# Mixers of a two-block network: the input is normalised once ahead of the projections, the matrix-memory mixer divides no more, and three products move to GpSimd

## The chip, the cores and the metric

The kernel runs on one core of one Trainium2 chip. A core has five engines, which the profile calls PE (TensorE; its weight loads are listed apart as PEld), DVE (VectorE), ACT (ScalarE), POOL (GpSimd) and SP (SyncE, which here issues the DMAs). Each engine works through its own instructions strictly in the order in which they were written, and waits on semaphores for the others. The metric is the device time of one execution in microseconds (us).

## What is computed

Two blocks of two layers each work on 256 tokens of width 1024, in float32. The change touches the mixers of the first block, which stand between two feed-forward layers in each of its two layers:

```python
u = rms_norm(x, mix_norm[l]) @ w_in[l]          # x * rsqrt(mean(x*x) + EPS) * g
u_ssd, u_ml, u_rw = jnp.split(u, ...)
y_ssd = ssd_mixer(u_ssd, ...)      # silu(conv(xbc)); y_diag = einsum(cb * decay_ls, x_dt); y * silu(z)
y_ml  = mlstm_mixer(u_ml, ...)     # h = num / max(|den|, exp(-m_t)); group_rms_norm(h * o, norm_g, H)
y_rw  = rwkv7_mixer(u_rw, ...)     # us = uf + (u_prev - uf) * shift_mu; decays, a = sigmoid(...), k, kk
x = x + jnp.concatenate([y_ssd, y_ml, y_rw], axis=-1) @ w_out[l]
```

The norm has no mean to subtract, so its factor for one token, `rsqrt(mean(x*x) + EPS)`, may be applied to x before the product with `w_in` or to each column of the product after it. Likewise the head's own norm in the mLSTM makes a factor per token on `h` cancel, but for EPS.

## The kernel before

Everything is laid out with features on the 128 partitions and the 256 tokens along them. A product with float32 accuracy is three products of rounded halves (`mm3`): each operand is split into a high and a low part (`wh`, `wl` of a weight tile, `xh`, `xl` of x), and `wh*xh + wh*xl + wl*xh` is summed in PSUM, so one output tile of 128 features by 256 tokens takes 24 matmuls (8 slices of the width, 3 each). A weight tile `wr` comes by DMA; ACT rounds it to `wh` (line 145, CAST), DVE subtracts it to `wl` (line 146). Three tiles `wh`, `wl` may stand ready.

`win` runs through the columns of `w_in` tile by tile. `prod` multiplies one tile into an accumulator; there are three accumulators `acc` in PSUM (`K.n_acc, K.n_m, K.n_pn = 3, 5, 0`), used in turn, so the fourth tile can begin when the first one's accumulator has been read. What reads it is code of the mixer concerned:

- 14 tiles for the RWKV mixer go through `shift`: DVE multiplies the product by `rb` (the norm's factor per token, broadcast to all partitions; tile `cvy`), ACT scales a copy by one token's shift (`pad`), DVE combines them (`cvt`, `kr` or `v`). The first two tiles are `wlal` and `sg`, then come k, r, v of four groups of heads;
- 10 tiles for the SSD and 4 for the mLSTM go through `conv` (`rb` into `pad` or `xm`, four taps, silu as `(tanh + 1) * y` with tanh in `cvt` and y in `cvy`);
- one narrow tile goes to `rows`, 8 tiles to `sz` (silu of z) and 4 to `o` (tanh).

x in `xh`, `xl` carries the gain but not `rb`: `rb` is known only when the norm's sums over all of x are, so the first product starts without it.

Beside `win`, in steps that are taken between its tiles, run the generators `rwkv` (`rwkv_prep`: decays, keys and the products `bk`, with `kf` on POOL; then the inverse in `rwkv_main`, with score matrices `A4`), then `ssd` and `mlstm`. In `ssd`, for each of eight pairs of heads f, `mask(f)` makes the decay scores (`rw,sel` and `negr,identr` on PE, four exponentials `sd<-m,na` of 128x128 on ACT, and the product with `cbT`, `sd<-sd,cbT` of 128x512), and `out(f)` the result (`sd,xdt` and `ec,st` on PE, `sy` on DVE, the gate `sz<-sy,sz` on POOL, its square `sq` on ACT, the sum `sacc` on POOL). Two tiles `sd` exist. In `mlstm`, the denominator is summed by a matmul with a matrix of ones, so that it stands on all 128 partitions, and is then made the divisor by max, reciprocal and product.

No scheduler moves instructions: the order on every engine is the order in which the generators are advanced. The two mixer stages lie at about 204 to 489 us (layer 0) and 864 to 1152 us (layer 1).

Of the kernel before, what the change touches and what calls it, by code (L numbers as in the profile page):

```python
# [10 lines left out]
F32R = mybir.dt.float32r  # L11
# [5 lines left out]
T = 256  # L17
# [3 lines left out]
EPS = 1e-6  # L21
# [182 lines left out]
class Kernel:  # L204
# [220 lines left out]

    def rows(self, l, ps, rb, S):

        with self.tc.tile_pool(name=f"rows{l}", bufs=1, reuse_waits="tile") as P:
            yield from self.rows_(l, ps, rb, S, P)
        S["rows"] = True  # L430

    def rows_(self, l, ps, rb, S, P):
        nc, PA = self.nc, self.p_ph
# [4 lines left out]
        n, h16, h4 = slice(0, 68), slice(0, 16), slice(0, 4)  # L438
        self.tt(x[n], ps[n], rb[n], ALU.mult)
        self.act(li[h4], x[32:36], AF.Identity, bias=self.col(f"bias{l}")[32:36])  # L440
        self.ts(x[n], x[n], self.col(f"bias{l}")[n], self.col("sgn")[n], ALU.add, ALU.mult)
        yield from wait(3)
# [65 lines left out]
        nc.vector.tensor_tensor_scan(mx[h4, 128:256], g[h4, 128:256], g[h4, 128:256], mp[h4], op0=ALU.max, op1=ALU.max)  # L508
        R4 = self.sb(P, [128, 640], "r4")
        self.ts(R4[h4, 0:256], mx[h4], -1.0, None, ALU.mult)  # L510
        self.tt(bc[h4], bc[h4], mx[h4], ALU.add)
        self.act(R4[h4, 256:512], bc[h4], AF.Exp, scale=-1.0)
        self.act(R4[h4, 512:640], mx[h4, 128:256], AF.Exp, scale=-1.0, bias=mp[h4])
        Rs = self.sb(self.p_ph, [128, 640], "r4s", 1, F32R)
        nc.gpsimd.memset(Rs.bitcast(F32), 0.0)
# [4 lines left out]
    def win(self, l, xh, xl, rb, S):  # L520
# [49 lines left out]
        rows = self.rows(l, S["ps"], rb, S)  # L570
        next(rows)
# [6 lines left out]
        for i in range(8):  # L578
            yield from prod()
            ps = S["ps"]  # L580
            th = self.sb(P, [128, T], "cvt", 2)
            u = self.sb(P, [128, T], "cvy", 2)
            self.tt(u, ps, rb, ALU.mult)
            self.act(th, u, AF.Tanh, scale=0.5)
            self.stt(S["sz"][:, i, :], th, 1.0, u, ALU.add, ALU.mult)
            yield
# [7 lines left out]
        for i in range(4):  # L594
            yield from prod()
            self.conv(l, 10 + i, S["ps"], rb, S["xm"][:, i, :], S["xc"][:, i, :])
            yield
        for i in range(4):
            yield from prod()
            u = self.sb(P, [128, T], "cvy", 2)  # L600
            self.tt(u, S["ps"], rb, ALU.mult)
            self.act(S["o"][:, i, :], u, AF.Tanh, scale=0.5)
            yield


    def ssd(self, l, S):
# [6 lines left out]
        with self.tc.tile_pool(name=f"ssd{l}", bufs=1, reuse_waits="tile") as P:  # L613
# [51 lines left out]
            def mask(f):  # L665
# [69 lines left out]
    def mlstm(self, l, S):  # L735
# [6 lines left out]
        with self.tc.tile_pool(name=f"ml{l}", bufs=1, side="right", reuse_waits="tile") as P:  # L742
# [4 lines left out]
            def s1(h):  # L747
                ps = self.misc()
                sel = self.sel[:, h:h + 1].to_broadcast([128, 128])
                self.mm(ps, sel, R4[:, 0:512], True, False)  # L750
                self.mm(ps[:, 0:256], self.identr, self.negr, False, True)
                wT = self.sb(P, [128, 2, 128], "wT")
                for c in range(2):
                    self.act(wT[:, c, :], ps[:, 128 * c:128 * c + 128], AF.Exp, bias=gc[:, c, h:h + 1])
                eb = self.sb(P, [128, T], "eb", 2)
                nc.scalar.copy(out=eb, in_=ps[:, 256:512])
                ps = self.misc()
# [119 lines left out]
    def rwkv_prep(self, l, S, PA, P):  # L877
# [12 lines left out]
        def prep(i):  # L890
# [58 lines left out]
    def rwkv_main(self, l, S, PA, P):  # L949
# [198 lines left out]
    def mixers(self, l, xh, xl, rb, feed):  # L1148
# [12 lines left out]
        with ExitStack() as es:  # L1161
# [869 lines left out]
```

## Time and profile before

| | before |
|---|---|
| median of 3 runs | 3082.5 us (3082.49 to 3082.59) |
| the profiled execution | 3082.42 us, of which the trace's span is 3080.7 us |
| PE busy | 3023.4 us, 98% of the span |
| DVE / ACT / POOL busy | 2173.9 us (71%) / 1255.4 us (41%) / 119.0 us (4%) |
| granted clock of TensorE, mean | 0.992 of full speed |

The 1.7 us between the profiled time and the span lie before the first and behind the last instruction of the trace. Busy times are sums of what the engines did; whether time is lost is told by PE's waits, since PE is busy nearly all the time.

### The profile page before, as it was taken

What the parts mean: (1) busy time and instruction counts of PE and PEld (TensorE: products, weight loads), DVE (VectorE), ACT (ScalarE), POOL (GpSimd) and SP (SyncE); (2) the same over time, 40 slices, a digit from 0 to 9 for tenths busy, and PEclk for the clock granted to TensorE, in tenths of its full rate; (3) what the DMA queues carried; (4) which work ended last, traced back from release to release, by engine and by line L of the source; (5) the groups of instructions that cost most, each with busy time, mean ns of one, the idle gap of its engine ahead of it and who ended that gap; (6) DMA issues with size and microseconds to landing.
All of it is one profiled execution on the core that took longest, in us unless ns stands there. A gap on an engine that the chain in (4) does not pass through costs nothing.

```text
span 3080.7 us, 53271 instructions
## 1 busy us (share of the span) xinstructions
PE 3023.4 (98%) x21561; PEld 2738.5 (89%) x21561; DVE 2173.9 (71%) x3726; ACT 1255.4 (41%) x2096; POOL 119.0 (4%) x192
## 2 busy tenths in 40 slices
PE   8999999999999999999999999999999999999998
PEld 8998989999998999988888888888888887899898
DVE  8989777767678778758988657886533336566665
ACT  5453455444453555532222442222322224444443
POOL 0000120000010210000000000000000001100000
PEclk9999999999999999999999999999999999999999
DMA  8773335565542335545755224664223223333455
GB/s 289 245 245 100 101 111 175 175 195 185 175 157 64 117 124 185 186 140 172 230 192 184 77 83 161 212 203 143 95 88 104 91 84 131 103 122 105 145 182 147
DMA packets 138487, 463.69 MB, mean 151 GB/s; under 512 B 15360, under 2 KB 15616, under 8 KB 137984
## 3 DMA queue, kind: packets, MB, share of 16 engines
q1 hardware_dynamic: 138240, 460.29, 46.4%
q8 instruction: 169, 2.77, 0.4%
q14 instruction: 78, 0.64, 0.1%
HBM read 459.18 MB, written 1.05 MB: 149 GB/s over the span
## 4 chain that ended last, share of the span: by engine, by line
PE 86%; issue 7%; DVE 3%; ACT 2%; POOL 1%; DMA 0%; POOLq 0%; SPq 0%; DVEq 0%; ACTq 0%
PE acc L214 80%; PE m L214 5%; ACT wh L145 1%; DVE wl L146 1%; PE pn L214 0%; POOL nr L228 0%; POOL rr L228 0%; DVE bk L225 0%; DVE sm L904 0%; POOL kf L228 0%; POOL sz L228 0%; DVE xl L225 0%; DVE sd L228 0%; DVE bk L228 0%; DMA wr<-gu 0%
## 5 line engine op out<-in xcount | busy, mean ns | idle before, releaser
L145 ACT CAST wh<-wr 128x1024 fp32r<-128x1024 f32 (+2 forms) x794 | 762.0, 961 | 1436.7 <-issue 710.4
L214 PE MATMUL acc<-xh,wh 128*128 128x256 f32 (+2 forms) x3776 | 1192.0, 318 | 13.6 <-ACT wh L145 10.0
L146 DVE TENSOR_TENSOR wl<-wr,wh 128x1024 fp32r<-128x1024 f32 (+2 forms) x794 | 885.2, 1115 | 441.6 <-ACT wh L145 440.1
L214 PE MATMUL acc<-xh,wl 128*128 128x256 f32 (+2 forms) x3776 | 1188.8, 316 | 3.6 <-DVE wl L146 3.6
L214 PE MATMUL acc<-xl,wh 128*128 128x256 f32 (+2 forms) x3776 | 1188.5, 315 | 0.6 <-DVE xl L225 0.6
L214 PEld LDWEIGHTS acc<-xh,wh 128*128 128x128 f32 (+1 forms) x3776 | 712.1, 190 | 70.2 <-ACT wh L145 10.8
L214 PEld LDWEIGHTS acc<-xh,wl 128*128 128x128 f32 (+1 forms) x3776 | 714.8, 189 | 56.8 <-DVE wl L146 5.0
L214 PEld LDWEIGHTS acc<-xl,wh 128*128 128x128 f32 (+1 forms) x3776 | 715.6, 190 | 52.0 <-DVE xl L225 1.1
L214 PE MATMUL acc<-hh,wh 128*128 128x256 f32 (+1 forms) x1537 | 491.7, 320 | 0.0
L214 PE MATMUL acc<-hh,wl 128*128 128x256 f32 (+1 forms) x1537 | 491.6, 320 | 0.0
L214 PE MATMUL acc<-hl,wh 128*128 128x256 f32 (+1 forms) x1537 | 491.6, 320 | 0.0
L389 DVE CUSTOM_DVE_ANT_0 adaj<-adaw,silur,cols 128x1024 bf16<-128x1024 f32 x288 | 368.5, 1279 | 10.9 <-DMA adaw<-ada 8.7
L214 PEld LDWEIGHTS acc<-hl,wh 128*128 128x128 f32 x1537 | 289.2, 188 | 24.1
L214 PEld LDWEIGHTS acc<-hh,wh 128*128 128x128 f32 x1537 | 289.2, 188 | 24.1
L214 PEld LDWEIGHTS acc<-hh,wl 128*128 128x128 f32 x1537 | 289.2, 188 | 23.9
L228 DVE TENSOR_TENSOR fh<-fh,acc 128x512 f32<-128x512 f32 (+1 forms) x88 | 54.6, 620 | 153.0 <-PE acc L214 152.0
L235 ACT CAST hh<-fh 128x256 fp32r<-128x256 f32 (+1 forms) x176 | 84.9, 482 | 22.4 <-DVE fh L228 21.3
L228 DVE TENSOR_TENSOR hl<-fh,hh 128x256 fp32r<-128x256 f32 (+1 forms) x176 | 91.2, 518 | 3.1 <-ACT hh L235 3.1
L228 POOL TENSOR_TENSOR nr<-nv,mhalf 128x2 f32<-128x2 f32 x18 | 16.7, 926 | 1873.6 <-DVE nv L232 616.1
L228 DVE TENSOR_TENSOR fgu<-acc,rb 128x256 f32<-128x256 f32 x176 | 66.4, 418 | 25.4 <-PE acc L214 25.4
L225 DVE SCALAR_TENSOR_TENSOR x<-acc,gg,x 128x256 f32<-128x256 f32 x56 | 27.0, 482 | 52.7 <-PE acc L214 52.7
L222 ACT ACTIVATE xh<-nf,m 128x256 fp32r<-128x256 f32 x88 | 41.6, 504 | 48.8 <-DVE nf L225 48.8
(417 smaller groups left out, 2980.7 us busy)
## 6 DMA issues: line engine op xcount, KB each, us to landing
wr<-gu SPq DMA_DIRECT2D x352, 512.0 KB, 3.5
adaw<-ada SPq DMA_DIRECT2D x144, 512.0 KB, 4.3
wr<-dn SPq DMA_DIRECT2D x128, 384.0 KB, 3.1
wr<-dn SPq DMA_DIRECT2D x128, 320.0 KB, 3.0
wr<-win SPq DMA_DIRECT2D x80, 512.0 KB, 3.5
wr<-rin SPq DMA_DIRECT2D x48, 512.0 KB, 3.5
wr<-wout SPq DMA_DIRECT2D x32, 512.0 KB, 3.5
wr<-rout SPq DMA_DIRECT2D x16, 512.0 KB, 3.5
```

The lines of the kernel that those rows point to most:

```text
L145: self.nc.scalar.copy(out=hi[:, 0:n], in_=t[:, 0:n])
L146: self.nc.vector.tensor_sub(out=lo[:, 0:n], in0=t[:, 0:n], in1=hi[:, 0:n].bitcast(F32))
L214: self.nc.tensor.matmul(out=out, lhsT=lhsT, rhs=rhs, start=start, stop=stop)
L222: self.nc.scalar.activation(out=out, in_=in_, func=func, **k)
L225: return self.nc.vector.scalar_tensor_tensor(out, in0, scalar, in1, op0=op0, op1=op1)
L228: return (eng or self.nc.vector).tensor_tensor(out, in0, in1, op=op)
L235: self.nc.scalar.copy(out=hi, in_=full)
L389: self.nc.vector.tensor_tensor_reduce(out=junk, in0=w, in1=self.silur[:, s, :], scale=0.5, scalar=b, op0=ALU.mult, op1=ALU.add, accum_out= ...
```

## The change

1. `normalise`, called behind the first product of `win`, writes normalised x, split into `xnh`, `xnl`: for each of the 8 slices one DVE product (x times gain times `rb`, tile `cvy`), one ACT rounding and one DVE subtraction. From the fifth tile on (the first v tile) the products read `xnh`, `xnl`, and the product with `rb` behind them is left out; where ACT or DVE read `cvy` before, they read the accumulator. In `conv` an ACT copy puts the product into `pad`.
2. In `conv`, silu's last product is an ACT pass (tanh + 1) and a POOL product in place of one DVE instruction.
3. The product `sd<-sd,cbT` and the two `bk<-kf,sm` go from DVE to POOL.
4. In the mLSTM the sum of the denominator is a matmul with one column of ones (tokens on partitions), `r4s` is 384 wide in place of 640, `exp(-m_t)` is transposed once for all heads (`ebc`), and `den` goes into the EPS of the head's norm, scaled, in place of dividing.
5. `A4` takes the places of `xh`, `xl`.

```diff
-    def conv(self, l, i, ps, rb, pad, dst):
+    def conv(self, l, i, ps, pad, dst):
...
-        self.tt(pad[:, 3:259], ps, rb, ALU.mult)
-        ps = pad[:, 3:259]
+        nc.scalar.copy(out=pad[:, 3:259], in_=ps)
...
-        self.stt(dst, th, 1.0, y, ALU.add, ALU.mult)
+        self.act(th, th, AF.Identity, bias=1.0)
+        self.tt(dst, th, y, ALU.mult, eng=nc.gpsimd)
...
     def shift(self, l, i, ps, rb, dst):
...
-        us = self.sb(self.p_ph, [128, T], "cvy", 2)
-        self.tt(us, ps, rb, ALU.mult)
+        us = ps
+        if rb is not None:
+            us = self.sb(self.p_ph, [128, T], "cvy", 2)
+            self.tt(us, ps, rb, ALU.mult)
...
+        xn = [self.sb(self.p_xn, [128, 8, T], t, 1, F32R) for t in ("xnh", "xnl")]
+        def normalise():
+
+            for k in range(8):
+                f = self.sb(P, [128, T], "cvy", 2)
+                self.stt(f, self.x[:, k, 0:T], self.col(f"mix_norm{l}", k), rb, ALU.mult, ALU.mult)
+                self.split(f, xn[0][:, k, :], xn[1][:, k, :])
+
...
+        x_ = xh, xl
         yield from prod()
+        normalise()
         us = self.sb(P, [128, T], "cvt", 2)
         self.shift(l, 12, S["ps"], rb, us)
...
             for dst, j in ((S["kr"][:, i, :, 0, :], 4 + i), (S["kr"][:, i, :, 1, :], i), (S["v"][:, i, :], 8 + i)):
+                if (i, j) == (0, 8):
+                    x_, rb = [[t[:, k, :] for k in range(8)] for t in xn], None
                 yield from prod()
...
-                self.tt(d, d, cbT[:, :, f // 4, :].unsqueeze(1).to_broadcast([128, 2, 2, 128]), ALU.mult)
+                self.tt(d, d, cbT[:, :, f // 4, :].unsqueeze(1).to_broadcast([128, 2, 2, 128]), ALU.mult, eng=nc.gpsimd)
...
-                self.mm(ps, sel, R4[:, 0:512], True, False)
+                self.mm(ps[:, 0:256], sel, R4[:, 0:256], True, False)
...
-                    o = slice(256 + 128 * c, 384 + 128 * c)
-                    self.mm(ps[:, o], self.cst("ones"), s["p"][:, c, :], True, c == 0)
+                    o = slice(256 + c, 257 + c)
+                    self.mm(ps[:, o], s["p"][:, c, :], self.cst("ones")[:, 0:1], True, c == 0)
...
-                nc.vector.reciprocal(den, den)
-                self.tt(den, den, ps[:, 0:256], ALU.mult)
-                self.stt(hs[:, h, :], S["o"][:, h, :], 1.0, den, ALU.add, ALU.mult)
+                self.stt(vs[:, 2 * h:2 * h + 2], den, 4 * EPS, den, ALU.mult, ALU.mult)
+                self.stt(hs[:, h, :], S["o"][:, h, :], 1.0, ps[:, 0:256], ALU.add, ALU.mult)
...
-                self.tt(bk[half[e], i, :, 1 - e, :], r4(kf)[half[e]], r4(em)[half[e]], ALU.mult)
+                self.tt(bk[half[e], i, :, 1 - e, :], r4(kf)[half[e]], r4(em)[half[e]], ALU.mult, eng=nc.gpsimd)
...
-        A4 = [self.sb(P, [128, 2, 2, 4, 128], t) for t in ("A0", "A1")]
+        A4 = [self.sb(self.p_x, [128, 2, 2, 4, 128], t) for t in ("xh", "xl")]
```

Where the instructions stand now. On DVE, at the start of the mixers of layer 0, where `nv` is the norm's variance and the next line the first weight tile behind it, before:

```order
L232 TENSOR_SCALAR nv<-m 128x2
L146 TENSOR_TENSOR wl<-wr,wh 128x1024
L228 TENSOR_TENSOR cvy<-acc,rb 128x256
L225 SCALAR_TENSOR_TENSOR cvt<-cvy,omm_120,pad 128x256
L228 TENSOR_TENSOR cvy<-acc,rb 128x256
```

and of the change, from the same `wl`:

```order
L146 TENSOR_TENSOR wl<-wr,wh 128x1024
L225 SCALAR_TENSOR_TENSOR cvy<-x,cols,rb 128x256 x2
L228 TENSOR_TENSOR xnl<-cvy,xnh 128x256 x2
L225 SCALAR_TENSOR_TENSOR cvy<-x,cols,rb 128x256 x2
L146 TENSOR_TENSOR wl<-wr,wh 128x1024
L228 TENSOR_TENSOR xnl<-cvy,xnh 128x256 x2
L225 SCALAR_TENSOR_TENSOR cvy<-x,cols,rb 128x256 x2
L146 TENSOR_TENSOR wl<-wr,wh 128x1024
L228 TENSOR_TENSOR xnl<-cvy,xnh 128x256 x2
L225 SCALAR_TENSOR_TENSOR cvy<-x,cols,rb 128x256 x2
L228 TENSOR_TENSOR xnl<-cvy,xnh 128x256 x2
L228 TENSOR_TENSOR cvy<-acc,rb 128x256 x2
```

All of `normalise` stands ahead of the first `cvy<-acc,rb`, which reads the accumulator of the first tile. On POOL, in the SSD of layer 0, before:

```order
L228 TENSOR_TENSOR xde<-xdt,de 128x512 x2
L228 TENSOR_TENSOR sz<-sy,sz 128x256 x2
L228 TENSOR_TENSOR sacc<-sacc,sq 128x256
L228 TENSOR_TENSOR sz<-sy,sz 128x256
L228 TENSOR_TENSOR sacc<-sacc,sq 128x256
```

and of the change, to the sixth head pair's product:

```order
L228 TENSOR_TENSOR sd<-sd,cbT 128x512 x2
L228 TENSOR_TENSOR sz<-sy,sz 128x256
L228 TENSOR_TENSOR sd<-sd,cbT 128x512
L228 TENSOR_TENSOR sz<-sy,sz 128x256
L228 TENSOR_TENSOR sacc<-sacc,sq 128x256
L228 TENSOR_TENSOR sz<-sy,sz 128x256
L228 TENSOR_TENSOR sd<-sd,cbT 128x512
L228 TENSOR_TENSOR sacc<-sacc,sq 128x256
L228 TENSOR_TENSOR sd<-sd,cbT 128x512
L228 TENSOR_TENSOR sz<-sy,sz 128x256
L228 TENSOR_TENSOR sacc<-sacc,sq 128x256
L228 TENSOR_TENSOR sd<-sd,cbT 128x512
```

The products `sd` stand between the gates `sz` and sums `sacc` of earlier pairs. On ACT the exponentials for the sixth pair (the second row of four) stand behind the square of the fourth pair's gate:

```order
L222 ACTIVATE sd<-m,na 128x128 x4
L222 ACTIVATE sq<-sz 128x256
L222 ACTIVATE sd<-m,na 128x128 x4
L222 ACTIVATE sacc<-sz 128x256
L222 ACTIVATE o<-acc 128x256
L145 CAST wh<-wr 128x1024
L222 ACTIVATE sd<-m,na 128x128 x4
```

ACT keeps this order of squares and exponentials from before; what is new is that POOL's gates and sums and the products `sd` are one queue.

## Rows read from the trace of the kernel before

**Rows 1.** The page: busy times by engine, and the granted clock in 40 slices.

```profile
PE 3023.4 (98%) x21561; PEld 2738.5 (89%) x21561; DVE 2173.9 (71%) x3726; ACT 1255.4 (41%) x2096; POOL 119.0 (4%) x192
...
PEclk9999999999999999999999999999999999999999
```

**Rows 2.** The page: the chain that ended last, by line.

```profile
PE acc L214 80%; PE m L214 5%; ACT wh L145 1%; DVE wl L146 1%; PE pn L214 0%; POOL nr L228 0%; POOL rr L228 0%; DVE bk L225 0%; DVE sm L904 0%; POOL kf L228 0%; POOL sz L228 0%; DVE xl L225 0%; DVE sd L228 0%; DVE bk L228 0%; DMA wr<-gu 0%
```

**Rows 3.** PE's waits, 200 to 500 us: for whom, us in total, times, longest.

```profile
PE m L214 <- POOL rr L228: 1.7, 3, 0.8
PE m L214 <- DVE vw L232: 1.1, 1, 1.1
PE m L214 <- DVE thw L225: 0.9, 2, 0.5
```

**Rows 4.** Windows, matmuls into `acc` alone: stretch, length, PE, PEld, DVE, ACT busy.

```profile
204.61:217.37 12.76, 12.76 (x108) 12.71 (x108) 2.09 (x5) 0.00 (x0) 1.00 0.51 174
```

**Rows 5.** Timeline of DVE, 205 to 207 us: start, duration, instruction, idle before.

```profile
205.33 1.23 DVE L146 TENSOR_TENSOR wl<-wr,wh 128x1024 fp32r<-128x1024 f32 x1 [2.03 <-ACT wh L145]
206.47 0.42 DVE L228 TENSOR_TENSOR cvy<-acc,rb 128x256 f32<-128x256 f32 x1
```

**Rows 6.** Timeline of ACT, 203 to 209 us.

```profile
205.21 0.37 ACT L1203 COPY rb<-m 128x256 f32<-128x256 f32 x1
```

**Rows 7.** Timeline of DVE, 1345 to 1350 us, the second block's norm.

```profile
1345.07 0.87 DVE L225 SCALAR_TENSOR_TENSOR nf<-x,gaf,acc 128x256 f32<-128x256 f32 x2 [1.28 <-PE acc L214]
1346.13 0.89 DVE L225 SCALAR_TENSOR_TENSOR xl<-nf,m,xh 128x256 fp32r<-128x256 f32 x2 [0.19 <-ACT xh L222]
1346.93 0.86 DVE L225 SCALAR_TENSOR_TENSOR nf<-x,gaf,acc 128x256 f32<-128x256 f32 x2
```

**Rows 8.** Windows: length, busy PE, PEld, DVE, ACT, POOL, granted clock (PEclk), DMA.

```profile
2185.00:2192.40 7.40, 5.33 (x46) 5.16 (x44) 3.57 (x8) 2.89 (x5) 1.68 (x1) 1.00 0.33 108
2192.40:2199.30 6.90, 6.02 (x28) 6.02 (x29) 6.66 (x18) 3.84 (x8) 0.70 (x1) 0.51 0.12 47
...
262.00:270.00 8.00, 7.57 (x73) 6.65 (x72) 7.50 (x18) 2.27 (x4) 0.20 (x2) 1.00 0.22 68
```

**Rows 9.** POOL's groups, 200 to 500 us: busy, mean ns, idle before.

```profile
L228 POOL TENSOR_TENSOR sz<-sy,sz 128x256 f32<-128x256 f32 x8 | 7.8, 970 | 25.7 <-DVE sy L225 25.7
L228 POOL TENSOR_TENSOR rr<-vv,mhalf 128x4 f32<-128x4 f32 x4 | 4.4, 1107 | 6.1 <-DVE vv L232 6.1
...
L228 POOL TENSOR_TENSOR kf<-kf,kr 128x256 f32<-128x256 f32 x4 | 2.9, 736 | 3.9 <-DVE kf L232 3.9
```

**Rows 10.** POOL's products of 128x512 in the second block.

```profile
L228 POOL TENSOR_TENSOR Dm<-De,De x8: 1282/1293/1572, 2579.6 to 2783.8; 128x512 f32<-128x512 f32 x8
```

**Rows 11.** DVE's groups, 200 to 500 us.

```profile
L228 DVE TENSOR_TENSOR cvy<-acc,rb 128x256 f32<-128x256 f32 x26 | 10.9, 420 | 6.5 <-PE acc L214 6.4
...
L228 DVE TENSOR_TENSOR sd<-sd,cbT 128x512 f32<-128x512 f32 x8 | 6.4, 798 | 2.2 <-ACT sd L222 2.2
```

**Rows 12.** Timeline of PE: first and last `sd,xdt`, and the wait behind.

```profile
396.11 0.66 PE L214 MATMUL m<-sd,xdt 128*64 128x128 f32 x8
...
416.87 0.66 PE L214 MATMUL m<-sd,xdt 128*64 128x128 f32 x8
...
421.72 0.46 PE L214 MATMUL m<-vw,kt 128*128 128x130 f32 x2 [1.12 <-DVE vw L232]
```

**Rows 13.** Timeline of ACT, 402 to 410 us, around one square.

```profile
407.68 0.42 ACT L222 ACTIVATE sq<-sz 128x256 f32<-128x256 f32 x1 [1.53 <-POOL sz L228]
408.00 1.12 ACT L222 ACTIVATE sd<-m,na 128x128 f32<-128x128 f32 x4
```

**Rows 14.** Timelines of POOL and DVE at 418 us.

```profile
418.42 1.74 POOL L228 TENSOR_TENSOR sz<-sy,sz 128x256 f32<-128x256 f32 x1 [0.52 <-DVE sy L225]
...
418.33 1.23 DVE L146 TENSOR_TENSOR wl<-wr,wh 128x1024 fp32r<-128x1024 f32 x1
```

**Rows 15.** PE's groups, 416 to 490 us, the mLSTM.

```profile
L214 PE MATMUL m<-r4s,sel 128*128 128x512 f32 x3 | 1.3, 420 | 0.0
```

More of the change, by code (lines that the diff above doesn't have):

```diff
@@ L424, in shift, with rows, rows_ @@
         self.stt(dst, f(us), self.omm[l][:, i:i + 1], f(pad[:, 0:256]), ALU.mult, ALU.add)
-    def rows(self, l, ps, rb, S):
+    def rows(self, l, ps, S):
         with self.tc.tile_pool(name=f"rows{l}", bufs=1, reuse_waits="tile") as P:
-            yield from self.rows_(l, ps, rb, S, P)
+            yield from self.rows_(l, ps, S, P)
         S["rows"] = True
-    def rows_(self, l, ps, rb, S, P):
+    def rows_(self, l, ps, S, P):
         nc, PA = self.nc, self.p_ph
@@ L438, in rows_ @@
         n, h16, h4 = slice(0, 68), slice(0, 16), slice(0, 4)
-        self.tt(x[n], ps[n], rb[n], ALU.mult)
-        self.act(li[h4], x[32:36], AF.Identity, bias=self.col(f"bias{l}")[32:36])
-        self.ts(x[n], x[n], self.col(f"bias{l}")[n], self.col("sgn")[n], ALU.add, ALU.mult)
+        self.act(li[h4], ps[32:36], AF.Identity, bias=self.col(f"bias{l}")[32:36])
+        self.ts(x[n], ps[n], self.col(f"bias{l}")[n], self.col("sgn")[n], ALU.add, ALU.mult)
         yield from wait(3)
@@ L508, in rows_ @@
         nc.vector.tensor_tensor_scan(mx[h4, 128:256], g[h4, 128:256], g[h4, 128:256], mp[h4], op0=ALU.max, op1=ALU.max)
-        R4 = self.sb(P, [128, 640], "r4")
+        R4 = self.sb(P, [128, 384], "r4")
         self.ts(R4[h4, 0:256], mx[h4], -1.0, None, ALU.mult)
         self.tt(bc[h4], bc[h4], mx[h4], ALU.add)
-        self.act(R4[h4, 256:512], bc[h4], AF.Exp, scale=-1.0)
-        self.act(R4[h4, 512:640], mx[h4, 128:256], AF.Exp, scale=-1.0, bias=mp[h4])
-        Rs = self.sb(self.p_ph, [128, 640], "r4s", 1, F32R)
+        self.act(bc[h4], bc[h4], AF.Exp, scale=-1.0)
+        self.act(R4[h4, 256:384], mx[h4, 128:256], AF.Exp, scale=-1.0, bias=mp[h4])
+        pt = self.misc()
+        for c in range(2):
+            nc.tensor.transpose(pt[:, 4 * c:4 * c + 4], bc[h4, 128 * c:128 * c + 128], ident[h4, h4])
+        eb = self.sb(self.p_ph, [128, 2, 4], "ebc")
+        nc.scalar.copy(out=eb.rearrange("p a b -> p (a b)"), in_=pt[:, 0:8])
+        R["eb"] = eb
+        Rs = self.sb(self.p_ph, [128, 384], "r4s", 1, F32R)
         nc.gpsimd.memset(Rs.bitcast(F32), 0.0)
@@ L535, in prod @@
             ps = self.acc()[0:m, 0:256]
+            xh, xl = x_
             for k in range(8):
@@ L545, in xbc @@
             pad = self.sb(P, [128, 260], "pad", 2)
-            self.conv(l, i, S["ps"], rb, pad, S["xs"][:, i, :] if i < 8 else S["bc"][:, i - 8, :])
+            self.conv(l, i, S["ps"], pad, S["xs"][:, i, :] if i < 8 else S["bc"][:, i - 8, :])
             yield
+        x_ = xh, xl
         yield from prod()
+        normalise()
         us = self.sb(P, [128, T], "cvt", 2)
@@ L569, in win @@
         yield from prod(68)
-        rows = self.rows(l, S["ps"], rb, S)
+        rows = self.rows(l, S["ps"], S)
         next(rows)
@@ L581, in win @@
             th = self.sb(P, [128, T], "cvt", 2)
[L582 to L585, printed above, removed]
+            self.act(th, ps, AF.Tanh, scale=0.5)
+            self.stt(S["sz"][:, i, :], th, 1.0, ps, ALU.add, ALU.mult)
             yield
@@ L595, in win @@
             yield from prod()
-            self.conv(l, 10 + i, S["ps"], rb, S["xm"][:, i, :], S["xc"][:, i, :])
+            self.conv(l, 10 + i, S["ps"], S["xm"][:, i, :], S["xc"][:, i, :])
             yield
@@ L599, in win @@
             yield from prod()
-            u = self.sb(P, [128, T], "cvy", 2)
-            self.tt(u, S["ps"], rb, ALU.mult)
-            self.act(S["o"][:, i, :], u, AF.Tanh, scale=0.5)
+            self.act(S["o"][:, i, :], S["ps"], AF.Tanh, scale=0.5)
             yield
@@ L754, in s1 @@
                     self.act(wT[:, c, :], ps[:, 128 * c:128 * c + 128], AF.Exp, bias=gc[:, c, h:h + 1])
-                eb = self.sb(P, [128, T], "eb", 2)
-                nc.scalar.copy(out=eb, in_=ps[:, 256:512])
                 ps = self.misc()
@@ L763, in s1 @@
                 self.act(k, ps[:, 256:512], AF.Copy, scale=128.0 ** -0.5)
-                st[h] = dict(wT=wT, eb=eb, q=q, k=k)
+                st[h] = dict(wT=wT, q=q, k=k)
             def sums(h, ps):
@@ L769, in sums @@
                     self.mm(ps[:, t:t + 1], q[:, 128 * t:128 * t + 128], self.cst("ones")[:, 0:1])
-                self.ts(vs[:, 2 * h:2 * h + 2], ps, 1.0 / 128, 4 * EPS, ALU.mult, ALU.add)
+                v = vs[:, 2 * h:2 * h + 2]
+                self.stt(v, ps, 1.0 / 128, v, ALU.mult, ALU.add)
             def s2(h):
@@ L778, in s2 @@
                 self.mm(ps[:, 256:384], xc[:, h, 0:128], wm[:, 4 + h, :])
-                self.mm(ps[:, 384:512], sel, R4[:, 512:640])
+                self.mm(ps[:, 384:512], sel, R4[:, 256:384])
                 v = self.sb(P, [128, 2, 128], "v", 2)
@@ L846, in mlstm @@
             r = self.sb(P, [128, 8], "mr")
+            self.ts(vs, vs, 1e-36, None, ALU.max)
             self.rsqrt(r, vs, 8)
@@ L1165, in mixers @@
             rwkv, ssd = self.rwkv(l, S), self.ssd(l, S)
-            for _ in self.win(l, xh, xl, rb, S):
-                more_of(rwkv)
-                more_of(ssd)
+            with self.tc.tile_pool(name=f"mixx{l}", bufs=1, side="right", reuse_waits="tile") as self.p_xn:
+                for _ in self.win(l, xh, xl, rb, S):
+                    more_of(rwkv)
+                    more_of(ssd)
             ml = self.mlstm(l, S)
```

8 lines of the change are left out of this document (4 added, 4 removed).

## The prediction

> **What bounds the kernel now.** I read the page first: PE is busy in 98% of the span at nearly full granted clock, and DVE comes next with 71% [rows 1]. The chain that ended last runs through PE's matmuls into `acc` (80%) and `m` (5%) [rows 2]. So a product taken from DVE is worth only a wait of PE that it ends, and a product put in front of something that PE needs costs what PE then waits. I read PE's waits in the mixers next: in layer 0 the longest are `rr` 1.7, `vw` 1.1 and `thw` 0.9 us, and with eight more of 0.9 or less they make some 8 us [rows 3]; layer 1 has the same list. That, and PE's own matmuls, is all that the change can win. Then I followed the two places where the new order puts work ahead of a product that PE waits for: the first tiles of `win`, and the SSD.
>
> **Part 1, `normalise`.** Today the tiles after the first run without any wait: from 204.61 to 217.37 us 108 matmuls begin, all of 12.76 us busy, 0.118 us each [rows 4]. The second and third tile take 48 of them, so the fourth begins at 204.61 + 48 x 0.118 = 210.3 us. It needs the accumulator of the first, which DVE releases with `cvy<-acc,rb`, begun at 206.47 [rows 5]: covered by 3.4 us. In the new order that instruction stands behind 8 products and 8 subtractions and two more `wl`. `rb` is ready at 205.21 + 0.37 = 205.58 [rows 6], DVE is in `wl` till about 206.5 (it begins at 205.33 and the next instruction at 206.47) [rows 5], so `normalise` begins at 206.5. The nearest rows are the norm of the second block, of the same form (two DVE products, two ACT roundings, two DVE subtractions, two buffers): 1345.07 to 1346.93, 1.86 us for two slices, with 0.19 us of waiting for ACT [rows 7]. Four such pairs are 7.4 us; less 0.4, since the subtraction here is a plain product-type instruction of 0.42 and not 0.48 us [rows 11]; the two `wl` add 2 x 1.14 and hide two of the waits, -0.4. Thus DVE is through at 206.5 + 7.4 - 0.4 + 2.3 - 0.4 = 215.4, `cvy<-acc,rb` ends 0.42 later [rows 11] and PE begins the fourth tile at about 216.0: it stands for 216.0 - 210.3 = **5.7 us**. If all four waits for ACT are hidden, 5.3; if none is, 6.1. Nothing else is ready for PE in that time, since its queue is in order.
>
> What this buys is some 10 products with `rb` in `shift`, 14 in `conv`, one in `rows`, 12 for z and o, each 0.42 us of DVE [rows 11], 37 x 0.42 = 15.5 us, against 8 x 0.9 = 7.2 put in. DVE is not the bound there, so I count only the waits that end on it: `thw` 0.9 and the few small ones; I take -0.5, between 0 and -2.5.
>
> **Clock.** PE's clock may fall behind such a gap. In the rows, a stretch of 7.40 us in which PE was busy 5.33 is followed by 6.90 us at a granted 0.51 of full speed, that is 1.2 in place of 2.4 GHz; a stretch of 8.00 with 7.57 busy stays at 1.00 [rows 8]. The new gap is longer than the 2 us of the first. A stretch of 6.9 us at half speed in which PE has work all the time does 3.4 us less of it: **+3.4 us**, or 0.
>
> **Part 2, the SSD's `sd` on POOL.** Today DVE takes 0.80 us on average [rows 11]. POOL takes 1.29 for a product of this size [rows 10], and 1.57 at worst; I take 1.38, between them, since DVE is at work beside it. The gates and sums cost POOL 0.73 undisturbed (as `kf`) and 0.97 on average (`sz`) [rows 9]. POOL's work for one head pair is then 1.38 + 0.73 + 0.73 = 2.84 us; PE passes from the first pair's result to the eighth's in 416.87 - 396.11 = 20.76 us [rows 12], 2.97 us a pair. By throughput alone POOL would keep up, and only the first pair would be late, by 1.38 - 0.80 = 0.6. But the queues are in order: ACT's exponentials for pair f + 2 stand behind the square of pair f's gate, and on POOL the next gate stands behind the next `sd`. So gate (0.73), square (0.42), four exponentials (1.12) [rows 13], `sd` (1.38) follow one another in a ring of 3.65 us, against 2.97; the sum `sacc` (0.73) hides beside the exponentials. Seven turns are 7 x 0.68 = 4.8 us. The wait for `vw` behind the last pair (1.12 us) [rows 12] is work of DVE and ACT that goes on meanwhile, so it falls away: 4.8 - 1.1 = **+3.7 us**. Below, 0 if the ring slips (some exponentials are ahead of the square) and throughput decides; above, 6, if ACT's `wh` and `o` fall into the ring too.
>
> The Trainium skill ("SBUF — State Buffer", section on who interferes with whom) says that a DVE instruction with two inputs in SBUF and a GpSimd instruction that reads SBUF share ports which one of them locks for its whole duration, so that the other stands. This case's trace agrees that they disturb each other: a gate `sz` beside DVE's `wl` took 1.74 us, and one undisturbed product 0.73 [rows 9, 14]. The rule speaks against this change.
>
> **Part 3, `bk` and silu on POOL.** Two `bk` of 64x256 stand ahead of `rr` on POOL, for which PE waits 1.7 us a layer [rows 3]; a product there takes 0.74. But POOL idles 6.1 us ahead of its four `rr`, until `vv` comes from DVE [rows 9], and eight `bk` need 8 x 0.74 = 5.9: they fit in on the whole, and `vv` comes up to 0.8 earlier (two products of at most 0.42 fewer ahead of it [rows 11]). The idle time is not spread evenly over the four, so the sum lies between -1.5 (nearly the whole wait goes) and +0.7 (one pair of `bk` that isn't hidden, 1.5 less 0.8). I take 0. Silu's ACT pass (0.42) and POOL product (0.73) stand beside tiles that take PE 2.84 us each, with no wait on them today: 0; if the inverse's matmuls come closer together for it, +1.5.
>
> **Part 4, mLSTM, and `A4`.** `r4s,sel` halves from 512 to 256 columns, by the 0.118 us of a matmul of 256 columns [rows 4] 4 x 0.12 = 0.5 us a layer (one of 512 is listed with 0.42 us of duration [rows 15]); columns of ones save little more, for the weights must still be loaded; two transposes come in. I take -0.7, between 0 and -1.0. DVE loses its four reciprocals, but PE doesn't wait for them now; the wait for the last root `mr` stays, POOL's root being the same. `A4` takes tiles that are last read in the fourth product, long before the scores: 0.
>
> **Sum per layer:** 5.7 + 3.4 + 3.7 + 0 - 0.7 - 0.5 = +11.6; two layers +23.2. From the profiled execution, 3082.4 (span 3080.7 and 1.7 around it; the median of the runs is 3082.5), that is 3105.6, say **3105 us**.
>
> **Rivals.** About 0.2% (6 us) is what a measurement of this kernel tells from no change: below 3076 is faster, above 3089 slower.
>
> - *Forecast, both stalls and a clock drop in each layer*, 0.46: 3105.
> - *Both stalls, the clock stays*: 2 x (11.6 - 3.4) = +16.4, 3099. For it: the rows' drops have other surroundings than this one. 0.24.
> - *Only `normalise` stalls, POOL keeps up in the SSD by throughput* (2.84 against 2.97): 2 x (5.7 - 1.2) = +9 without a drop, +16 with one, 3091 to 3098. 0.10.
> - *POOL and DVE block each other in the SSD*: gates stretched from 0.73 to 1.74 [rows 9, 14] make the ring 1.0 longer, 7 us more a layer, 3119. Today only some gates are that long (mean 0.97). 0.08. This is what the skill's rule named above would bring if each product met a two-input DVE instruction.
> - *The wait merely changes its place*: `normalise`'s 5.7 us are met by the waits of today falling away almost whole (8 us a layer), within 0.2%: 0.07.
> - *Faster: DVE's relief wins.* The place is PE's waits of [rows 3]; price 8 us a layer and 0.7 of PE's work, 2 x (5.3 - 8.7) = -7, 3075 to 3076 at best, if POOL and the clock cost nothing. It decides from where the stall at the fourth tile is under the waits saved; against it, most of these waits are for POOL (`rr`, `mr`), which gets more to do. If the accumulator of the first tile were read before `normalise`, there would be no stall at all, but the order says otherwise. 0.05.
>
> So slower 0.88, same 0.07, faster 0.05. The range leaves out the last two and most of the fourth: 3088 to 3116, which also takes in the bounds of each term (5.3 with POOL hidden and the waits gone, 5.3 - 1.0 - 1.3 = 3, twice +6; up to 2 x (6.1 + 3.4 + 6 + 1.5) = +34).
>
> **What would show it.** In the changed profile PE waits 5 to 6 us for DVE `cvy` ahead of the fourth tile, once in each layer, and the granted clock is near 0.5 in the stretch behind; PE's waits for `sd` are with POOL and sum to about 4 us a layer; `vw` is gone from the list; `sd` takes 1.3 to 1.6 us on POOL. I am wrong if PE's wait at the fourth tile is under 3 us, if `sd` on POOL takes under 1 us, or if the waits of today (`rr`, `mr`, `thw`) vanish together.

## The result and the profile after

The changed kernel takes 3115.5 us (median of 4 runs, 3111.9 to 3120.7) where before takes 3082.5: a ratio of 1.011 with a 95% interval of 1.0096 to 1.0124, 33 us more. The forecast was 3105 us, and the result lies at the upper edge of its range (3088 to 3116): two of the four executions are above it. The direction was right, and the size by a third too small. The profiled execution took 3116.4 us, its span is 3114.6 us. Two single executions of later runs are left out of all ratios, one of 3332.2 us at a mean granted clock of 0.833 and one of 7024.4 us.

On the page PE's busy time is 7.5 us longer than in [rows 1], the span 33.9 us; DVE lost 44 us of work and POOL gained 55, half of what it had again:

```profile
PE 3030.9 (97%) x21565; PEld 2746.8 (88%) x21565; DVE 2130.1 (68%) x3618; ACT 1273.1 (41%) x2162; POOL 174.5 (6%) x252
```

PE's waits in the mixers of layer 0 (200 to 520 us; us in total, times, longest), to be set against [rows 3]:

```profile
PE m L214 <- POOL sd L228: 5.2, 4, 2.1
PE acc L214 <- DVE cvy L228: 5.1, 1, 5.1
PE m L214 <- POOL pad L419: 2.0, 1, 2.0
PE m L214 <- DVE vv L232: 1.8, 3, 1.0
PE m L214 <- POOL rr L228: 1.7, 1, 1.7
PE m L214 <- POOL mr L228: 1.4, 1, 1.4
PE m L214 <- DVE bk L225: 1.3, 1, 1.3
PE m L214 <- DVE vw L232: 1.0, 1, 1.0
PE m L214 <- ACT wh L145: 1.0, 1, 1.0
```

With two small ones these are 21 us against 8 before; layer 1 has 20. Two are new and were forecast, `cvy` and `sd`. The third group wasn't: the waits of the preparation (`pad`, which is the root `rr` under the name of what follows it on POOL, `rr`, `vv`, `bk`, `wh`) make 7.8 us in place of some 4.5. `vw` was to vanish and hasn't. In both layers together the waits grew by 25.7 us, and PE's busy time by 7.5 with four instructions more of 21561, which fits matmuls at a lower clock; the two make nearly all of the 33.9 us.

The first wait, on DVE's timeline (start, duration). `normalise` begins at 206.06, and the read of the first accumulator comes at 214.64, as the walk from [rows 5 to 7] had it (206.5 and 215.4):

```profile
204.91 1.23 DVE L146 TENSOR_TENSOR wl<-wr,wh 128x1024 fp32r<-128x1024 f32 x1 [2.02 <-ACT wh L145]
206.06 0.88 DVE L225 SCALAR_TENSOR_TENSOR cvy<-x,cols,rb 128x256 f32<-128x256 f32 x2
207.01 0.83 DVE L228 TENSOR_TENSOR xnl<-cvy,xnh 128x256 fp32r<-128x256 f32 x2
...
213.90 0.82 DVE L228 TENSOR_TENSOR xnl<-cvy,xnh 128x256 fp32r<-128x256 f32 x2
214.64 0.75 DVE L228 TENSOR_TENSOR cvy<-acc,rb 128x256 f32<-128x256 f32 x2
```

What it brings, in windows of the same execution (length, PE, PEld, DVE, ACT, POOL busy, granted clock). PE does nothing from 210.1 to 215.2, and then works for five microseconds at half clock (granted 0.50, that is 1.2 in place of 2.4 GHz). The granted clock also falls behind the preparation's waits (0.72 on average from 256 to 262) and twice in the SSD (0.66 in 410 to 415 and 431 to 436):

```profile
210.00:215.00 5.00, 0.09 (x1) 0.00 (x0) 4.93 (x13) 2.46 (x5) 0.00 (x0) 0.83 0.58 206
215.00:220.00 5.00, 4.80 (x22) 4.83 (x23) 2.38 (x7) 3.47 (x8) 0.30 (x3) 0.50 0.01 4
...
256.00:262.00 6.00, 5.14 (x33) 4.97 (x34) 2.91 (x6) 1.93 (x4) 0.96 (x3) 0.72 0.25 87
...
410.00:415.00 5.00, 5.00 (x39) 4.27 (x36) 2.10 (x3) 2.67 (x7) 2.77 (x3) 0.66 0.15 43
...
431.00:436.00 5.00, 5.00 (x32) 4.34 (x30) 0.48 (x1) 1.87 (x7) 3.08 (x4) 0.66 0.23 92
```

In the preparation a timeline of POOL, and below it one of DVE, show what stretches. For two of the four groups of heads `thw` takes 1.05 us beside the two `bk` on POOL, which take 1.59 us; for the other two `thw` takes 0.49 and 0.48 and the two `bk` 1.67 and 1.91. The root `rr` now stands behind `bk`; two of the four take 1.07 us, and the two that run beside DVE's `wl` take 2.04 and 1.87 (mean 1.51, where [rows 9] have 1.11):

```profile
227.86 1.59 POOL L228 TENSOR_TENSOR bk<-kf,sm 64x256 f32<-64x256 f32 x2
...
254.76 2.04 POOL L228 TENSOR_TENSOR rr<-vv,mhalf 128x4 f32<-128x4 f32 x1
...
267.94 1.91 POOL L228 TENSOR_TENSOR bk<-kf,sm 64x256 f32<-64x256 f32 x2
```

```profile
227.80 1.05 DVE L225 SCALAR_TENSOR_TENSOR thw<-kr,cols,kf 128x256 f32<-128x256 f32 x1 [0.85 <-POOL kf L228]
...
252.72 0.49 DVE L225 SCALAR_TENSOR_TENSOR thw<-kr,cols,kf 128x256 f32<-128x256 f32 x1 [0.85 <-POOL kf L228]
...
254.73 1.21 DVE L146 TENSOR_TENSOR wl<-wr,wh 128x1024 fp32r<-128x1024 f32 x1
```

In the SSD PE's timeline, against [rows 12]: from the first pair's result to the eighth's 435.92 - 409.64 = 26.3 us in place of 20.8, and `vw` is still waited for:

```profile
409.64 0.66 PE L214 MATMUL m<-sd,xdt 128*64 128x128 f32 x8 [2.06 <-POOL sd L228]
...
430.80 0.66 PE L214 MATMUL m<-sd,xdt 128*64 128x128 f32 x8 [1.82 <-POOL sd L228]
435.92 0.66 PE L214 MATMUL m<-sd,xdt 128*64 128x128 f32 x8
440.69 0.46 PE L214 MATMUL m<-vw,kt 128*128 128x130 f32 x2 [1.04 <-DVE vw L232]
```

On POOL the products `sd` take 1.26 to 1.38 us and the gates between them 0.72 to 0.74, so the rival in which POOL and DVE block each other in the SSD did not come.

One sentence of the text on the kernel must be put right: the order is not simply the one in which the generators advance. The experiment with `normalise` in pieces has one of its products ahead of a `cvt` that is written before it, and in the changed kernel the second `cvy<-acc,rb` stands ahead of the first `cvt`; so something moves instructions when the kernel is built, and what does is not shown. The orders shown are what was built, and no number rests on that sentence.

### The profile page after: what moved, and what is told of

It reads as the page before. It is cut to its first block, busy times and chain, and to the rows that moved or that the text cites. A ratio compares the mean times of both kernels' runs of the same rounds, so it can differ in the third digit from the quotient of the medians.

```text
span 3114.6 us, 53331 instructions
## 1 busy us (share of the span) xinstructions
PE 3030.9 (97%) x21565; PEld 2746.8 (88%) x21565; DVE 2130.1 (68%) x3618; ACT 1273.1 (41%) x2162; POOL 174.5 (6%) x252
## 3 DMA queue, kind: packets, MB, share of 16 engines
HBM read 459.18 MB, written 1.05 MB: 148 GB/s over the span
## 4 chain that ended last, share of the span: by engine, by line
PE 85%; issue 7%; DVE 3%; POOL 2%; ACT 2%; DMA 0%; POOLq 0%; SPq 0%; DVEq 0%; ACTq 0%
PE acc L214 79%; PE m L214 5%; DVE wl L146 1%; ACT wh L145 1%; PE pn L214 0%; POOL bk L228 0%; POOL sd L228 0%; POOL rr L228 0%; POOL nr L228 0%; DVE xl L225 0%; DVE cvy L225 0%; ACT sd L222 0%; POOL sz L228 0%; DVE sm L920 0%; DVE x L225 0%
## 5 line engine op out<-in xcount | busy, mean ns | idle before, releaser
L214 PE MATMUL acc<-xh,wh 128*128 128x256 f32 (+1 forms) x3184 | 1017.6, 323 | 24.1 <-DVE cvy L228 10.2
L214 PE MATMUL acc<-xh,wl 128*128 128x256 f32 (+1 forms) x3184 | 1020.4, 322 | 3.0 <-DVE wl L146 3.0
L214 PE MATMUL acc<-xl,wh 128*128 128x256 f32 (+1 forms) x3184 | 1021.0, 322 | 0.7 <-DVE xl L225 0.6
L214 PEld LDWEIGHTS acc<-xh,wh 128*128 128x128 f32 x3184 | 602.9, 191 | 74.9 <-ACT xnh L235 10.6
L214 PEld LDWEIGHTS acc<-xh,wl 128*128 128x128 f32 x3184 | 605.6, 190 | 53.5 <-DVE wl L146 4.1
L214 PEld LDWEIGHTS acc<-xl,wh 128*128 128x128 f32 x3184 | 606.4, 191 | 50.3 <-DVE xl L225 1.3
L214 PE MATMUL acc<-xnh,wh 128*128 128x256 f32 (+1 forms) x592 | 177.7, 300 | 0.0
L214 PE MATMUL acc<-xnh,wl 128*128 128x256 f32 (+1 forms) x592 | 170.3, 288 | 0.0
L214 PE MATMUL acc<-xnl,wh 128*128 128x256 f32 (+1 forms) x592 | 169.5, 286 | 0.0
L214 PEld LDWEIGHTS acc<-xnl,wh 128*128 128x128 f32 (+1 forms) x592 | 112.4, 190 | 1.9 <-issue 0.3
```

The lines of the kernel that those rows point to most:

```text
L214: self.nc.tensor.matmul(out=out, lhsT=lhsT, rhs=rhs, start=start, stop=stop)
```

## The experiments

Ratios are to the kernel before on the same chip, with 95% intervals; a difference of two ratios is given with the uncertainty that the two intervals make together. Where the chip differed, before itself had 3079 to 3081 us.

**Decay product back on DVE** (one step undone):

```diff
-...to_broadcast([128, 2, 2, 128]), ALU.mult, eng=nc.gpsimd)
+...to_broadcast([128, 2, 2, 128]), ALU.mult)
```

> The changed kernel with the SSD's decay product back on DVE, all else as changed (3115.5 us). The theory of the forecast (a ring of waits through POOL, 3.7 us a layer, and nothing else): 3115.5 - 7.4 = 3108 us. Rival (each of the two long waits for POOL in the SSD also brings a stretch at half clock, so that the place costs what the trace shows from the first head pair's result to the last, 7.4 us a layer): 3115.5 - 14.8 = 3100.7 us, and no drop of the granted clock between the first and the last head pair. If POOL were not the cause, PE's waits for sd would stay at 5.2 us a layer.

Measured 3110.4 us (3102.5 to 3116.1), 1.0093 (1.0078 to 1.0107). That is 5.2 us less than the changed kernel, uncertain by 6: the forecast's 7.4 fits, the rival's 14.8 doesn't. The wait for `sd` fell from 5.2 to 2.2 us a layer, not to the 0.6 of before, and `vw` stayed at 1.0. What stays of `sd` is mostly silu's: with silu on DVE as well it is 0.9 (below). The six executions are 14 us apart, and their mean granted clock goes with the time (0.990 in the two of 3102.5 and 3102.9 us, 0.987 in the three above 3112). So from here on waits are read from traces.

**`bk` back on DVE**:

```diff
-... r4(kf)[half[e]], r4(em)[half[e]], ALU.mult, eng=nc.gpsimd)
+... r4(kf)[half[e]], r4(em)[half[e]], ALU.mult)
```

> The changed kernel with the two bk products of each head group back on DVE. Forecast's theory (POOL's idle time takes them up): no difference, 3115 us. Rival (POOL's products hold up DVE's thw and kr beside them, and rr comes later): the waits for thw, rr and bk fall back to those of before, 2.5 to 4 us a layer, 3107 to 3110 us, and thw takes 0.48 us in place of 1.05.

Measured 3114.0 us, 1.0097 (1.0082 to 1.0111): the time doesn't tell the two theories apart. The groups of 200 to 290 us do, and so do the waits of the preparation, 6.2 us (0.4 of it for `G`) in place of 7.8. The changed kernel has `thw` with 769 ns on average and `rr` with 1512; here they are back at 485 and 1007:

```profile
L228 POOL TENSOR_TENSOR rr<-vv,mhalf 128x4 f32<-128x4 f32 x4 | 6.0, 1512 | 0.3
...
L225 DVE SCALAR_TENSOR_TENSOR thw<-kr,cols,kf 128x256 f32<-128x256 f32 x4 | 3.1, 769 | 3.4 <-POOL kf L228 3.4
```

```profile
L225 DVE SCALAR_TENSOR_TENSOR thw<-kr,cols,kf 128x256 f32<-128x256 f32 x4 | 1.9, 485 | 3.4 <-POOL kf L228 3.4
...
L228 POOL TENSOR_TENSOR rr<-vv,mhalf 128x4 f32<-128x4 f32 x4 | 4.0, 1007 | 1.8 <-DVE vv L232 1.8
```

**`normalise` in four pieces**, each behind a tile's shift, the normalised input used from the sixth tile on:

```diff
-        def normalise():
-            for k in range(8):
+        def normalise(k0):
+            for k in (k0, k0 + 1):
...
-        normalise()
         us = self.sb(P, [128, T], "cvt", 2)
         self.shift(l, 12, S["ps"], rb, us)
+        normalise(0)
...
         self.shift(l, 13, S["ps"], rb, us)
+        normalise(2)
...
-                if (i, j) == (0, 8):
+                if (i, j) == (1, 5):
...
                 self.shift(l, j, S["ps"], rb, dst)
+                if (i, j) in ((0, 4), (0, 0)):
+                    normalise(4 if j else 6)
```

> The changed kernel with normalise cut into four pairs of slices, one behind each of the first four tiles' shift, and the normalised input used from the sixth tile on (one product with rb more). If the wait at the fourth tile is for the accumulator that stands behind normalise: that wait (5.1 us a layer) and the half clock behind it (2 to 2.5) vanish, 3115.5 - 15 = 3100 us. Rival (DVE has too much to do there in any order, and the wait moves to the tiles behind): 3108 to 3112 us, with PE waiting for xnl or cvy at the fifth to seventh tile.

Measured 3096.5 us, 1.005 (1.0038 to 1.0062). The wait of 5.1 us is gone (0.2 for `xnl` is left), and with it the half clock behind it (granted 1.00 from 205 to 230 us): 0.006 x 3082 = 18.5 us, uncertain by 6. The rival falls.

**All three**: the ratio is 1.0011 (1.0002 to 1.0019), 3084.7 us.

> The three together: decay product and bk back on DVE, normalise in four pieces. If the costs are separate and sum: 3115.5 - 15 - 15 - 6 = 3079 us, just under the kernel before (3082.5), by the relief of DVE and the lighter mLSTM. Rival (what is left of the change costs too, silu's product on POOL above all): 3084 to 3090 us.

So even with these three places mended the change gains nothing, as the rival had it. For its trace one more execution was profiled, with 3089.8 us:

> The version with all three steps back and silu on POOL once more, for a trace beside that of the one with silu on DVE. If silu on POOL costs by waits, PE's waits in a layer's mixers are 2 to 4 us above the 5.9 us of that other version; if only by the clock, the waits are the same and stretches of half clock show in it.

Its waits are 9.3 us a layer, 3.4 above the 5.9 of the version with silu on DVE, so silu on POOL costs by waits; stretches at half clock show as well (0.53 from 270 to 275 us).

**`sd` and `bk` back, `normalise` whole**, and then the same with the gap filled:

> The changed kernel with decay product and bk on DVE, normalise whole at its place. The two single steps back gave a ratio to before of 1.0093 (decay product) and 1.0097 (bk), against 1.011. If their waits simply sum (3.0 us a layer in the SSD and 1.6 in the preparation by the two traces): 1.011 less 2 x 4.6 / 3082 = 1.008, about 3106 us on a chip where before has 3081. Rival (the clock decides more than the waits): between 1.004 and 1.010, with the times of one kernel spread over more than 8 us.

Measured 3106.4 us, 1.008 (1.0067 to 1.0093), as by the sum.

```diff
+                if (i, j) == (0, 0):
+                    pf = self.misc()
+                    for _ in range(43):
+                        self.mm(pf[:, 0:256], self.identr, self.negr)
```

> The kernel before this one in the list, with 43 matmuls of 128x256 whose result nobody reads (constants, into a misc tile) between the third and the fourth tile of win: PE works through the 5.1 us in which it would wait for the accumulator. If the half clock behind the fourth tile comes from that gap: no granted clock of 0.5 in the 10 us behind, and 2 x 2.5 = 5 us less than without them, ratio about 0.0016 lower. Rival (the clock falls for another reason, or the added work comes on top of the wait): the same time or up to 10 us more.

Measured 3099.6 us, 1.0061 (1.0048 to 1.0073), 5.9 us less with 86 matmuls more, uncertain by 5.5. Windows without them:

```profile
210.00:215.00 5.00, 0.95 (x9) 0.75 (x7) 4.93 (x11) 2.34 (x5) 0.00 (x0) 0.90 0.47 141
215.00:220.50 5.50, 4.44 (x21) 4.47 (x22) 3.25 (x9) 3.60 (x9) 0.30 (x3) 0.50 0.16 63
```

and with them:

```profile
210.00:216.00 6.00, 6.00 (x53) 6.00 (x52) 5.93 (x12) 3.27 (x8) 0.00 (x0) 1.00 0.51 160
216.00:222.00 6.00, 5.93 (x50) 5.75 (x49) 3.71 (x11) 4.29 (x10) 0.30 (x3) 1.00 0.15 57
```

So the half clock behind this gap comes from PE's own idleness. What it costs is some 2.2 us a gap by the trace without them: 22 matmuls behind it take 4.8 us, at 0.118 us each they would take 2.6. The 5.9 us are not the price of the two gaps alone: in the profiled executions another slow stretch of layer 0 (0.50 from 280 to 285 us) is gone too with the gap filled, although the waits ahead of it are the same.

**Silu in one DVE instruction again**, on the version with all three:

```diff
-        self.act(th, th, AF.Identity, bias=1.0)
-        self.tt(dst, th, y, ALU.mult, eng=nc.gpsimd)
+        self.stt(dst, th, 1.0, y, ALU.add, ALU.mult)
```

> The version with all three steps back (decay product and bk on DVE, normalise in four pieces; ratio 1.0011) and silu's last product on DVE in one instruction too, as before. If silu's products on POOL lie beside PE's work for nothing: the same, 1.001. Rival (they hold up DVE and ACT and lengthen waits in the preparation): 2 to 4 us less, ratio 0.9995 to 1.0005, at or under the kernel before.

Measured 3076.2 us, 0.9987 (0.9978 to 0.9996): faster than before, and 0.0024 x 3082 = 7.4 us faster than with silu's product on POOL. PE's waits of a layer are 5.9 us in place of 9.3, and no stretch of half clock is left in the mixers of the profiled execution. The 3.4 us a layer make 6.8 of the 7.4; the largest parts are `sd` and `bk`, with silu on POOL

```profile
PE m L214 <- DVE sd L228: 2.2, 4, 1.2
...
PE m L214 <- DVE bk L225: 1.3, 1, 1.3
```

and in one DVE instruction:

```profile
PE m L214 <- DVE sd L228: 0.9, 3, 0.3
...
PE m L214 <- DVE bk L225: 0.6, 1, 0.6
```

**Each step alone in the kernel before:**

> The kernel before with the mLSTM's part of the change alone (no division, narrow r4s, column sums). Forecast's theory: PE's work shrinks by 0.7 us a layer, ratio 0.9995. Rival: the wait for the root mr, 0.4 to 0.5 us longer in the changed kernel, takes it back: 1.000.

The mLSTM's part: 3075.1 us, 0.9984 (0.9975 to 0.9993), 5 us less: the fastest version measured, level with the one above within the intervals. The one above holds this part too, so the normalised input, even with `normalise` in pieces, gains nothing that can be told.

> The kernel before with silu's last product alone as an ACT pass and a POOL product (14 a layer). Forecast: no difference, 1.000. Rival, from the version with all three steps back (1.0011 with it on POOL, 0.9987 with it on DVE): 7 us more, 1.0024, with longer waits of PE in the preparation and the inverse, where these tiles run.

Silu: 1.0001 (0.9992 to 1.001). Alone it costs nothing that can be measured, though its waits are 9.6 us in layer 0 in place of 7.9, most of it for `sd` (2.1 in place of 0.6).

> The kernel before with the SSD's decay product alone on POOL. Forecast: 3.7 us a layer, 7.4 us in all, 1.0024, with the wait for vw gone. Rival, from the changed kernel's trace (waits of 5.2 us a layer, vw's wait not gone, and one or two stretches at half clock behind them): 9 to 15 us, 1.003 to 1.005.

The decay product: 1.004 (1.0026 to 1.0054), 12.3 us, more than the forecast's 7.4 and within the rival. The waits for `sd` are 4.9 us a layer in place of 0.6, those for `vw` 1.1 as before, and in each layer the clock falls once (0.85 and 0.81 in 415 to 425 us).

> The kernel before with the two bk products alone on POOL. Forecast: no difference, 1.000 (bounds -3 to +1.4 us for both layers). Rival (POOL's products stand in the way of DVE's thw, kr and the root rr): 3 to 7 us, 1.001 to 1.0023, with thw near 1.05 us where bk runs beside it.

`bk`: 1.0007 (0.9998 to 1.0016), not told from nothing; but PE's waits for `thw` are 3.4 us a layer and those for `rr` and `pad` 2.8, together 6.2 where before has 3.2 for these three, and `thw` takes 913 ns on average. Other waits went, so that all together are 9.4 us in layer 0 in place of 7.9.

**What of silu costs**, tried on the version with all three undone (1.0011 with the product on POOL, 0.9987 with one DVE instruction). First the pass on ACT, with the product on DVE:

> The version with all three steps back, with silu's (tanh + 1) as a pass on ACT and the product on DVE: ACT's work of the change without POOL's. With the product on POOL the ratio was 1.0011, with one DVE instruction 0.9987. If POOL's product is what costs: 0.9987, and no DVE bk pair of 1.4 us. If the ACT pass costs: 1.0005 to 1.001.

Measured 1.001 (1.0002 to 1.0019), as with POOL; PE's waits are 7.8 us a layer. Then POOL's product without a reader:

```diff
         self.stt(dst, th, 1.0, y, ALU.add, ALU.mult)
+        self.tt(self.sb(self.p_ph, [128, T], "scr"), th, y, ALU.mult, eng=nc.gpsimd)
```

> The version with silu's product on DVE (0.9987), and beside it the same product on POOL once more into a tile that nobody reads, 14 a layer. No engine waits for its result; only its use of SBUF and the two buffers that it reads are added. If POOL's products cost by standing in DVE's way: ratio 1.000 to 1.001, and DVE instructions beside them stretched (bk pair 1.4 us in place of 0.86). If they cost only where their result is waited for: 0.9987.

Measured 1.0006 (0.9997 to 1.0015), 6 us above the version without it, uncertain by 4, although nobody waits for its result; PE's waits are 8.3 us a layer in place of 5.9. The last `bk` pair shows one place, on DVE's timeline without POOL's products:

```profile
262.64 0.86 DVE L225 SCALAR_TENSOR_TENSOR bk<-sq,sm 64x256 f32<-64x256 f32 x2
```

and with this product on POOL, on DVE's timeline and on POOL's:

```profile
263.85 1.40 DVE L225 SCALAR_TENSOR_TENSOR bk<-sq,sm 64x256 f32<-64x256 f32 x2
...
263.55 0.96 POOL L228 TENSOR_TENSOR scr<-cvt,cvy 128x256 f32<-128x256 f32 x1 [1.53 <-ACT cvt L222]
```

PE's wait for `bk` is 1.1 us there in place of 0.6. So both halves of silu's edit cost there, the pass on ACT and the product on POOL, and what they cost does not sum (7.1 and 5.9 us, together 7.4).

**Four accumulators** in the changed kernel:

```diff
-        K.n_acc, K.n_m, K.n_pn = 3, 5, 0
+        K.n_acc, K.n_m, K.n_pn = 4, 4, 0
```

> The changed kernel with four accumulators and four misc tiles in place of three and five. If PE's wait of 5.1 us at the fourth tile is for an accumulator: the fourth tile begins without a wait, the fifth waits for the first accumulator's read, some 2.3 us (5.1 less 2.84 of one tile) a layer, or for the last slice of the normalised input, 1 to 2 us more; 5 to 10 us less in all, ratio 1.008 to 1.0095, if four misc tiles cost nothing elsewhere. If the wait is for DVE in another way, it stays at the fourth tile.

Measured 1.0113 (1.0097 to 1.0128), no gain. But the wait has moved to the fifth tile and shrunk from 5.1 to 3.4 us, so it is one for an accumulator:

```profile
216.27 0.35 PE L214 MATMUL acc<-xnh,wh 128*128 128x256 f32 x1 [3.42 <-DVE cvy L228]
```

That the ratio did not fall stays without a shown cause. Its difference to the changed kernel's is uncertain by 6 us, so a gain of 5 isn't excluded; and in the profiled execution, the shortest of the four with 3109.8 us, PE's waits in the mixers of both layers are 5.3 us shorter than in the changed kernel's.

## Why the forecast was too low

Right was **part 1**: 5.7 us a layer forecast at the fourth tile, 5.1 measured. The accumulators and the clock were each shown to be the cause by a run of its own (four accumulators, the filled gap). The clock's term was put at 3.4 and is some 2.3 (23 matmuls in 5.0 us in place of 2.7): by the granted 0.83 of 210 to 215 us the slow stretch begins at about 213.3 and ends at 220.1, as long as the one in [rows 8], but 1.9 us of it fall into the wait. By the trace part 1 and the clock are thus 2 x 7.4 = 14.8 us where 18.2 was forecast; that the four pieces gave 18.5, uncertain by 6, is so near the forecast by luck.

**Part 2** was right in mechanism and too small: 3.7 us a layer forecast, 6.1 measured by the product alone (12.3 in two layers). The ring itself was sized well: 4.8 us a layer forecast, 4.3 more waiting measured. Its term "the wait for `vw` ... falls away" (-1.1) is wrong: PE takes `vw` 4.8 us behind the last pair's result before and after, so that wait moves with it. And its waits bring slow stretches of their own, worth about 1.7 us a layer with the product alone, where the sum had one only at the fourth tile.

The step that failed is **part 3**, "`bk` and silu on POOL", "I take 0". Undone in the changed kernel, silu was worth 7.4 us (as the last step) and `bk`, by the waits, 1.6 us a layer: 10.6 us in all, where the sum fell short by 10.7 (33.9 by the ratio less 23.2). The working asked only whether POOL had the time (idle 6.1 us, work 5.9) and not what its products do beside those of DVE: `thw` from 0.48 to 1.05 us, a `bk` pair on DVE from 0.86 to 1.40, and roots, pushed back until `wl` runs beside them, from 1.07 to 2.04. The rule weighed in part 2, from the Trainium skill ("SBUF — State Buffer", section on who interferes with whom), says that of a DVE instruction with two inputs in SBUF and a GpSimd one that reads SBUF the second to come stands until the first is through. It was priced for the SSD, where `sd` and the gates show next to nothing of it, and left out of part 3, where the rows above agree that the two hinder each other. Nor did the working ask what the longer path through ACT does: the pass on ACT alone costs as much as both halves (1.001), and that is no meeting of POOL and DVE.

The product without a reader shows a cost of POOL's work apart from any wait for its result. What was not tried is the same POOL work without its reads of SBUF; and that product also holds the buffers `cvt` and `cvy` longer, which stays open as a second cause.

**Part 4** was too small on the side of gain: -0.7 us a layer forecast, -2.5 measured alone (interval -1.1 to -3.9). In its trace `vw` is waited for 0.5 us in place of 1.1 and `Rt` no more; `mr` 1.4 in place of 0.9, where one more DVE instruction stands ahead of the root; the rest is not located. DVE's relief (-0.5) was wrong to be counted: in the changed kernel the waits of the preparation got longer, and no version shows a gain from it. The lower end of the range took 1.3 us a layer for saved waits, where the working's own bounds allow 4.0 (2.5 and 1.5); the result doesn't hang on it.

By steps undone: `normalise`'s place 18.5 us (1.011 to 1.005), `sd` and `bk` 12.0 (to 1.0011), silu 7.4 (to 0.9987), and the rest gains 4.0; 18.5 + 12.0 + 7.4 - 4.0 = 33.9. Each difference is uncertain by 4 to 6 us, so that they close is no proof of each. Silu's 7.4 against nothing alone says that the parts don't simply add. By the waits silu costs 3.4 us a layer on the mended version and 1.7 alone (layer 0); the wait for `sd` grows in both (by 1.3 and 1.5), those for `bk` and `vw` only in the mended version (by 0.7 and 0.5). Why they don't when silu stands alone is not shown.

## What to carry to other kernels

An engine's idle time says whether it can take work, not what that work does to its neighbour: before moving a product to GpSimd, look in the trace at what DVE does beside it and price that stretched. Work written ahead of the read that frees an accumulator costs as much as the ring has no tiles left to cover; cut it into pieces behind the reads. On a kernel that keeps PE busy, count for a new gap like the 5.1 us of this one also the slow stretch behind it, less what of that stretch falls into the gap.

## What was not expected of the hardware

86 matmuls that compute nothing made the kernel 5.9 us faster (1.008 to 1.0061, uncertain by 5.5 us), the granted clock staying at 1.00 where it was 0.50. And versions with more waits tend to spread more from execution to execution: the standard deviation is 6.0 us over six with the decay product on DVE, and 1.8 over eleven with the mLSTM's part alone.
